# Delta stage of a hybrid decoder layer: a second tile for the output gate, the inverse's 64-blocks in turns, query norms from matmuls with ones

## The chip, the cores and the metric

The kernel runs on one core of one Trainium2 chip. The metric is device time in microseconds (us), the median of three runs. Engines are named as in the profile: PE is TensorE's matmuls, PEld its weight loads, DVE is VectorE, ACT ScalarE, POOL GpSimd, and SP the engine that issues most DMAs. Each engine works through its own instructions in order and waits on semaphores for the others.

## The reference

One layer in fp32 on 1024 prompt rows and 8 single decode rows: a combined projection, a gated delta rule (8 heads of 128, chunks), sliding-window attention, two gated branches, and a convolutional feed-forward net. What the change touches is the delta rule of the prompt:

```python
q = _l2norm(q) * (GDN_DK ** -0.5)
k = _l2norm(k)
...
m = jnp.where(strict, jnp.einsum('bhnik,bhnjk->bhnij', kb, k) * gam, 0.0)
t_inv = lax.linalg.triangular_solve(eye + m, jnp.broadcast_to(eye, m.shape),
                                    left_side=True, lower=True, unit_diagonal=True)
...
def step(S, inp):
    u_n, w_n, a_n, qd_n, kd_n, last_n = inp
    v_new = u_n - jnp.einsum('bhck,bhkv->bhcv', w_n, S)
    o = jnp.einsum('bhck,bhkv->bhcv', qd_n, S) + jnp.einsum('bhij,bhjv->bhiv', a_n, v_new)
    S = S * last_n[..., None, None] + jnp.einsum('bhck,bhcv->bhkv', kd_n, v_new)
    return S, o
```

The output o is RMS-normed and multiplied by silu of an output gate, which is one more projection.

## The kernel before

The kernel has five stages: start (to 90 us), attention (to 406), the delta rule (to 1125), the branches (to 1420) and the feed-forward net (to 2084). Every large product is one `mm`: three matmuls (L180, L181, L182) of split operands (wh, wl for the weights, b1h, b1l for the activations), 384 or 264 columns each. DVE makes wl (L130) and ACT wh (L129).

The delta stage uses chunks of 128 rows, so a head h of 8 has 8 chunks n. For each head three generators run:

- `delta_prepare`: K and Q transposed on PE (L190, `tp<-ident,K`, `tp<-ident,Q`), four transposes a burst, two bursts for each. ACT squares each transposed chunk and sums it along the free axis (L888, `osq`), which gives the squared norms `n2`. DVE scales the transposed K into `kd` (L890). Then the products K K and Q K (L906, L907), and V transposed and scaled into `vn` (L918).
- `unit_inverse`: the inverse `W` of each chunk's unit triangular matrix. Blocks of 16 are inverted by a loop on DVE (L1019, L1020, tile `T`), go through DRAM (`T<-wd`), and are turned by DVE (L1034, `MR`). Then the blocks are joined on PE: to 32 by L1038 and L1044 (quarters of 32x32), to 64 by L1056 and L1061, to 128 by L1070 and L1074 (64x64 blocks). L1070 fills the PSUM tile `zp` for all eight chunks, ACT copies it to `Zb` (L1071), L1074 fills `qp`, and ACT copies that into `W` (L1075).
- `delta_scan`: a chain over n. A step is `rc<-S,K` (L947, PE), `y` (L948, DVE), `rc<-y,W` (L950, PE), `s` (L952, ACT), `rc<-s,kd` (L954, PE), and the new S (L963, DVE); beside it L957 and L958 add up `o`. After n = 3 and n = 7 ACT squares four chunks of o (L969), DVE and POOL make a factor of the sums (L971, L972, and `power` at L125), DVE writes the normed o over `vn` (L976), PE turns vn (L190, `rc<-ident,vn`, "the turning of vn"), and DVE multiplies it into the gate's tile `sg` (L983), which SP stores to `oa` (L988).

Beside these run projections as filler: `delta_gate(h)` (an mm into th, then `sg`, L858 and L859), `delta_project(h + 2)` (mm, then the conv of K, Q and V on DVE: L784 once, L786 three times for each, L792 twice, with a tanh on ACT, L791), and projections of the branch gates. `weave` (L1258) gives each generator priorities: the inverse from 0, the scan from 100, delta_prepare of the next head from 250, filler from 100000. The program's scheduler then places each instruction on its engine by these priorities, by when its inputs are ready in its own model of time, and by when a tile's room is free; what it chooses is fixed, and each engine runs its list in order. `sg` has one buffer for heads 0 to 6, and head 7 borrows the room of a `z` tile. A pool's room is fixed for its life; constants that are not in `KEPT` are in the pool `cp2`, which lives on.

Of the kernel before, what the change touches and what calls it, by code (L numbers as in the profile page):

```python
# [12 lines left out]
AF = mybir.ActivationFunctionType  # L13
ALU = mybir.AluOpType
# [4 lines left out]
P = 128  # L19
NP = 1024  # L20
NS = 8
NT = NP + NS
KC = 8
H = 8
NCH = 8
FT = 22
CONV_W = 3072
EPS = 1e-6
# [5 lines left out]
HALF = [(0, 512), (512, 520)]  # L34
QW = 260
KEPT = {"ident", "ones", "mhalf", "phalf", "vecs", "fcw", "mT", "a2"}
COL_GATE, COL_BETA, COL_SQ = 3072, 4096, 4112
COL_SK, COL_SV, COL_GA, COL_GB = 5136, 5392, 5648, 6672


def bc(ap, dim, n):

    a = ap.unsqueeze(dim)
    shape = list(a.shape)
    shape[dim] = n
    return a.broadcast_to(shape)
# [18 lines left out]
class Step:  # L65
# [28 lines left out]
        return pool.tile(shape, dt, tag=tag, name=f"{tag}_{self.n}", **kw)  # L94

    def const(self, shape, name, dt=F32):
        pool = self.cp if name in KEPT else self.cp2
        return pool.tile(shape, dt, tag=name, name=name)


# [749 lines left out]
    def delta_gate(self, pa, pool, h):  # L850

        nc = self.nc
        sg = self.t(pool, [P, NT], "sg", bufs=1) if h + 1 < H else self.t(self.pz, [P, NT + 3], "z")[:, :NT]

        def gate_out(t, ps):
            lo, n = PARTS[t]
            th = self.t(pa, [P, 512], "th", bufs=2)[:, :n]
            nc.scalar.activation(th, ps, AF.Tanh, scale=0.5)  # L858
            nc.vector.scalar_tensor_tensor(sg[:, lo:lo + n], th, 1.0, ps, op0=ALU.add, op1=ALU.mult)  # L859

        self.project(self.win(COL_GATE + h * P), self.h, gate_out)
        nc.gpsimd.tensor_copy(self.sgs[:, h, :], sg[:, NP:NT])
        self.sg[h] = sg
        yield

    def delta_prepare(self, pool, psum, h):
        nc = self.nc
        K, Q, V = self.kqv[h]
# [45 lines left out]
        for c0 in (0, 4):  # L914
            tp = self.t(psum, [P, 4, P], "tp", bufs=2)
# [74 lines left out]
    def unit_inverse(self, pool, psum, h, U):  # L990

        nc, W = self.nc, self.W
# [7 lines left out]
        for p in range(4):  # L1000
            c = slice(16 * (p % 2), 16 * (p % 2) + 16)
# [8 lines left out]
        U64, Zb = UZ[0:64], UZ[64:128]  # L1010
# [12 lines left out]
        for p in range(4):  # L1023
            q, c = 16 * (p % 2) + 8 * (p // 2), slice(16 * (p % 2), 16 * (p % 2) + 16)
# [5 lines left out]
        TT = self.t(pool, [P, 2, NCH, 32], "MR", bufs=1)  # L1030
# [4 lines left out]
        zp = self.t(psum, [P, NCH, 32], "tp", bufs=2)  # L1035
# [5 lines left out]
        qp = self.t(psum, [P, NCH, 32], "tp", bufs=2)  # L1041
# [24 lines left out]

        nc.vector.transpose(flat(TT[32:64, 0]), flat(w01))
        zp = self.t(psum, [P, NCH, 2, 32], "tp", bufs=2)
        for n in range(NCH):
            nc.tensor.matmul(zp[64:128, n], U64[:, n, :], TT[0:64, :, n, :], start=True, stop=True)  # L1070
        nc.scalar.copy(Zb, zp[64:128].rearrange("p n a i -> p n (a i)"))  # L1071
        qp = self.t(psum, [64, NCH, 64], "tp", bufs=2)
        for n in range(NCH):
            nc.tensor.matmul(qp[:, n, :], Zb[:, n, :], W[64:128, n, 64:128], start=True, stop=True)  # L1074
        nc.scalar.copy(W[0:64, :, 64:128], qp)  # L1075


    def conv_states(self, pool, psum):
# [872 lines left out]

    def run(self):
        S, nc = ExitStack, self.nc
        self.constants()
        with S() as ca:
            with S() as c:
                pool, psum = self.pool("p2", 1, ctx=c), self.pool("q2", 1, PSUM, ctx=c)
                for tag, bufs in dict(qst=8, raw=2, kh=2, kl=2, E=3, obt=2, pp=2, pc=2, o=2).items():
                    self.bufs[id(pool), tag] = bufs
# [33 lines left out]
            with S() as c:  # L1993
                pa, pool, psum = self.pool("pa", 1, ctx=c), self.pool("p4", 1, ctx=c), self.pool("q4", 1, PSUM, ctx=c)
# [27 lines left out]
        with S() as c:  # L2022
            pool2, pool = self.pool("p6b", 1, ctx=c), self.pool("p6", 1, ctx=c)
# [48 lines left out]
```

## Time and profile before

| | us |
|---|---|
| median of three runs | 2083.78 |
| the runs | 2090.38, 2083.78, 2079.47 |
| span of the profiled execution | 2084.4 |
| PE busy in the span | 2012.7 |
| DVE busy | 1347.8 |
| ACT busy | 900.2 |
| POOL busy | 520.2 |

The profile is of one execution. A group's row has the line, engine and operation, out<-in by tile names, shape and count, then busy us and the mean ns of one, then the idle time of the engine just before its instructions and what ended it. A row of the timeline has start, duration, line and count of a run of like instructions, and in brackets the idle time before and what released it. Durations of pipelined matmuls overlap; from start to start is what one costs. An fp32 matmul is two records in the profile (x2) and one row in the order below.

### The profile page before, as it was taken

The page shows a single profiled execution, that of the slowest core. Times are in us where ns is not written, and L with a number is a line of the kernel's source. Part 1 is how long each engine was busy: PE and PEld are TensorE (multiplying, and loading weights), DVE is VectorE, ACT ScalarE, POOL GpSimd, SP SyncE. Part 2 cuts the span into 40 slices and gives each one's busy share as a digit, 9 for nine tenths or more (in the row PEclk, how much of TensorE's full clock was granted, in tenths as well). Part 3 has the DMA queues.
Part 4 walks back from the last instruction along what each step waited for, and adds up shares of the span by engine and source line. Part 5 has one row for each costly group of instructions (what it writes and reads, how often), then busy time and mean ns, then how long its engine had stood idle before and what let it go on. Part 6 is the DMA issues. An engine that isn't in the chain of part 4 may idle for free.

```text
span 2084.4 us, 41297 instructions
## 1 busy us (share of the span) xinstructions
PE 2012.7 (97%) x16245; PEld 1910.2 (92%) x16245; DVE 1347.8 (65%) x2714; ACT 900.2 (43%) x2233; POOL 520.2 (25%) x594
## 2 busy tenths in 40 slices
PE   7999998999999999989989999999999999999897
PEld 4987877799999999989989999999999999999897
DVE  5755768473655647656544675578876776767756
ACT  4664545433344243432342542354444444534443
POOL 2000000121321221201111000005575466446421
PEclk9999999999999999999999999999999999999999
DMA  8256443331332322312275855323333333488862
GB/s 300 62 144 210 135 167 116 117 94 51 80 80 61 73 72 52 89 42 62 63 223 172 285 186 163 112 63 97 105 91 112 102 92 112 136 305 266 291 215 94
DMA packets 301887, 275.75 MB, mean 132 GB/s; under 512 B 59730, under 2 KB 248111, under 8 KB 301676
## 3 DMA queue, kind: packets, MB, share of 16 engines
q1 hardware_dynamic: 295642, 252.14, 39.6%
q0 software_dynamic: 5552, 20.37, 2.8%
q8 instruction: 127, 2.08, 0.4%
q14 instruction: 68, 0.56, 0.1%
q10 hardware_dynamic: 498, 0.61, 0.1%
HBM read 212.93 MB, written 62.51 MB: 132 GB/s over the span
## 4 chain that ended last, share of the span: by engine, by line
PE 83%; DVE 5%; DMA 5%; ACT 3%; issue 1%; SPq 1%; POOL 1%; DVEq 0%; POOLq 0%; ACTq 0%
PE mm L180 19%; PE mm L181 18%; PE mm L182 18%; PE wv L180 3%; PE wv L182 3%; PE wv L181 3%; PE wy L182 2%; PE wy L180 2%; PE wy L181 2%; PE pv L652 1%; PE pt L190 1%; PE tp L190 1%; DVE x L1472 1%; PE mm L264 1%; PE rc L954 1%
## 5 line engine op out<-in xcount | busy, mean ns | idle before, releaser
L180 PE MATMUL mm<-b1h,wh 128*128 128x384 f32 (+1 forms) x1520 | 496.9, 328 | 3.7 <-ACT gt L1294 1.6
L181 PE MATMUL mm<-b1l,wh 128*128 128x384 f32 (+1 forms) x1520 | 489.3, 323 | 0.0
L182 PE MATMUL mm<-b1h,wl 128*128 128x384 f32 (+1 forms) x1520 | 488.0, 323 | 0.3 <-DVE wl L130 0.3
L180 PEld LDWEIGHTS mm<-b1h,wh 128*128 128x128 f32 x1520 | 286.7, 189 | 12.4 <-issue 4.6
L181 PEld LDWEIGHTS mm<-b1l,wh 128*128 128x128 f32 x1520 | 287.1, 189 | 4.4 <-issue 3.1
L182 PEld LDWEIGHTS mm<-b1h,wl 128*128 128x128 f32 x1520 | 286.3, 189 | 3.9 <-issue 2.8
L129 ACT ACTIVATE wh<-raw 128x1024 fp32r<-128x1024 f32 x83 | 87.0, 1049 | 122.4 <-PE mm L181 70.2
L130 DVE TENSOR_TENSOR wl<-raw,wh 128x1024 fp32r<-128x1024 f32 x82 | 101.0, 1233 | 57.2 <-ACT wh L129 55.1
L181 PE MATMUL mm<-pk,w 128*128 128x260 f32 (+1 forms) x440 | 124.8, 284 | 1.1 <-DVE pk L130 1.1
L180 PE MATMUL mm<-pk,w 128*128 128x260 f32 (+1 forms) x440 | 124.8, 284 | 0.0
L182 PE MATMUL mm<-pk,w 128*128 128x260 f32 (+1 forms) x440 | 124.5, 283 | 0.0
L130 DVE TENSOR_TENSOR w<-ws,w 128x512 fp32r<-128x512 f32 x88 | 78.0, 886 | 36.9 <-ACT w L129 36.7
L1626 ACT COPY bml<-mm 128x256 f32<-128x256 f32 (+1 forms) x132 | 48.9, 371 | 100.6 <-PE mm L182 96.7
L180 PE MATMUL mm<-bmh,w 128*128 128x260 f32 (+1 forms) x320 | 90.3, 282 | 0.0
L182 PE MATMUL mm<-bmh,w 128*128 128x260 f32 (+1 forms) x320 | 90.1, 282 | 0.0
L1681 DVE SCALAR_TENSOR_TENSOR fa<-fz,fcw,fa 128x512 f32<-128x512 f32 x88 | 75.2, 874 | 18.2 <-ACT fa L1679 17.9
L180 PE MATMUL mm<-b2h,wh 128*128 128x384 f32 (+1 forms) x256 | 83.2, 328 | 2.9 <-ACT wh L129 2.8
L181 PEld LDWEIGHTS mm<-pk,w 128*128 128x128 f32 x440 | 83.2, 189 | 1.3 <-DVE pk L130 1.3
L181 PE MATMUL mm<-b2l,wh 128*128 128x384 f32 (+1 forms) x256 | 83.6, 327 | 0.4 <-DVE b2l L130 0.4
L180 PEld LDWEIGHTS mm<-pk,w 128*128 128x128 f32 x440 | 83.2, 189 | 0.2 <-ACT bml L1626 0.2
L182 PEld LDWEIGHTS mm<-pk,w 128*128 128x128 f32 x440 | 83.4, 190 | 0.0
L182 PE MATMUL mm<-b2h,wl 128*128 128x384 f32 (+1 forms) x256 | 82.8, 326 | 0.0
(645 smaller groups left out, 5886.2 us busy)
## 6 DMA issues: line engine op xcount, KB each, us to landing
raw<-in_w_in_dram SPq DMA_DIRECT2D x59, 512.0 KB
ws<-in_w_ffn_down_dram SPq DMA_DIRECT2D x55, 256.0 KB
raw<-xd SPq DMA_DIRECT2D x47, 258.0 KB
raw<-in_w_ffn_down_dram SPq DMA_DIRECT2D x47, 256.0 KB
raw<-in_w_ffn_gate_dram SPq DMA_DIRECT2D x22, 512.0 KB
raw<-in_w_ffn_up_dram SPq DMA_DIRECT2D x22, 512.0 KB
qst<-in_w_mod_dram SPq DMA_DIRECT2D x16, 512.0 KB
raw<-in_w_mod_dram SPq DMA_DIRECT2D x16, 512.0 KB
```

Source lines behind the costliest of these rows:

```text
L129: self.nc.scalar.activation(hi, x, AF.Copy)
L130: (eng or self.nc.vector).tensor_tensor(lo, x, hi.bitcast(F32), op=ALU.subtract)
L180: mm(ps, whi, xhi, start=first, stop=False, **kw)
L181: mm(ps, whi, xlo, start=False, stop=False, **kw)
L182: self.last_mm = mm(ps, wlo, xhi, start=False, stop=last, **kw).ins
L190: self.nc.tensor.transpose(out, in_, self.ident[:p, :p])
L264: nc.tensor.matmul(ps[32 * j:32 * j + 32], self.cT[:, k0 + j, :], ws[j // 2][:, j % 2, :], start=k0 == 0, stop=k0 > 0)
L652: nc.tensor.matmul(pv[64 * r:64 * r + 64], V[:, n - back, ch], ps[:, r::2, :], start=back == 0, stop=back == (n > 0))
L954: yield step(nc.tensor.matmul(ds, kd[:, n, :], s, start=True, stop=True))
L1472: nc.vector.scalar_tensor_tensor(x[:, :np_], ps[:, :np_], by[:, j, 8:9], x[:, :np_], op0=ALU.mult, op1=ALU.add)
L1626: self.last_copy = nc.scalar.copy(r[p, i], x[p])
L1681: nc.vector.scalar_tensor_tensor(ai[:, c:e], zi[:, j + c:j + e], col(j), ai[:, c:e], op0=ALU.mult, op1=ALU.add)
```

## The change

It has three parts.

1. `sg` gets two buffers for all heads (L851 and its tile). The room comes from ten constants (`SHORT`), which go into a new pool `cp1` that closes after the attention.
2. In `delta_prepare`, the norms of Q no longer come from eight transposes. For four chunks at a time ACT squares Q as it lies (128 x 512, into the tile `ed`), four matmuls with a 128x32 part of `ones` sum it over the partitions, each for 32 of the rows of every chunk and onto its own 32 partitions, DVE turns the 32x32 blocks (128 x 128) and adds the small constant into `n2`. K's norms stay as they were.
3. In `unit_inverse`, L1070's and L1074's blocks are issued by fours: four chunks of zp, then four times a chunk of zp and one of qp in turn, then four of qp, with a copy for each four. `issue_after` keeps the second and third groups behind the copy before them.

```diff
+SHORT = {"triu", "tril", "trilu", "stril", "sink", "qs", "kx", "vx", "zero", "a1"}
...
-        pool = self.cp if name in KEPT else self.cp2
+        pool = self.cp if name in KEPT else self.cp1 if name in SHORT else self.cp2
...
-        sg = self.t(pool, [P, NT], "sg", bufs=1) if h + 1 < H else self.t(self.pz, [P, NT + 3], "z")[:, :NT]
+        sg = self.t(pool, [P, NT], "sg", bufs=2)
...
-        for a, src in ((0, K), (1, Q)):
-            for c0 in (0, 4):
-                tp = self.t(psum, [P, 4, P], "tp", bufs=2)
-                for c in range(4):
-                    self.transpose(tp[:, c, :], src[:, c0 + c, :])
-                junk = self.t(pool, [P, P], "osq", bufs=1)
-                for c in range(4):
-                    nc.scalar.activation(junk, tp[:, c, :], AF.Square, accum_out=n2[:, a, c0 + c:c0 + c + 1])
-                if a == 0:
-                    nc.vector.tensor_tensor(kd[:, c0:c0 + 4, :], tp, bc(self.edd[:, h, c0:c0 + 4], 2, P), op=ALU.mult)
-                yield
-        nc.vector.tensor_scalar_add(n2, n2, 4 * EPS)
...
+        nc.vector.tensor_scalar_add(n2[:, 0], n2[:, 0], 4 * EPS)
+        for c0 in (0, 4):
+            q2 = self.t(pool, [P, 4, P], "ed", bufs=1)
+            nc.scalar.activation(q2, Q[:, c0:c0 + 4, :], AF.Square)
+            sums = self.t(psum, [P, 4, 32], "tp", bufs=2)
+            for j in range(4):
+                r = slice(32 * j, 32 * j + 32)
+                nc.tensor.matmul(sums[r], self.ones[:, 0:32], q2[:, :, r], start=True, stop=True)
+            turned = self.t(pool, [P, 4, 32], "osq", bufs=1)
+            nc.vector.transpose(turned.rearrange("p n i -> p (n i)"), sums.rearrange("p n i -> p (n i)"))
+            nc.vector.tensor_scalar_add(n2[:, 1, c0:c0 + 4], turned[:, :, 0], 4 * EPS)
+            yield
...
-        for n in range(NCH):
-            nc.tensor.matmul(zp[64:128, n], U64[:, n, :], TT[0:64, :, n, :], start=True, stop=True)
-        nc.scalar.copy(Zb, zp[64:128].rearrange("p n a i -> p n (a i)"))
         qp = self.t(psum, [64, NCH, 64], "tp", bufs=2)
-        for n in range(NCH):
-            nc.tensor.matmul(qp[:, n, :], Zb[:, n, :], W[64:128, n, 64:128], start=True, stop=True)
-        nc.scalar.copy(W[0:64, :, 64:128], qp)
+        copied = None
+        for c0 in (0, 4, 8):
+            with self.tc.issue_after(copied) if copied else nullcontext():
+                for n in range(c0, c0 + 4):
+                    if n < NCH:
+                        nc.tensor.matmul(zp[64:128, n], U64[:, n, :], TT[0:64, :, n, :], start=True, stop=True)
+                    if c0:
+                        nc.tensor.matmul(qp[:, n - 4, :], Zb[:, n - 4, :], W[64:128, n - 4, 64:128], start=True, stop=True)
+            if c0 < NCH:
+                copied = nc.scalar.copy(Zb[:, c0:c0 + 4], zp[64:128, c0:c0 + 4].rearrange("p n a i -> p n (a i)")).ins
+            if c0:
+                nc.scalar.copy(W[0:64, c0 - 4:c0, 64:128], qp[:, c0 - 4:c0])
...
+                self.cp1 = self.pool("cp1", 1, ctx=c)
+                self.constants()
```

The scheduler's choice changes with it, in the delta stage only. Lines of the changed kernel: L180 to L182 become L181 to L183, L190 L191, L784 L785, L786 L787, L792 L793, L947 L957, L948 L958, L950 L960, L954 L964, L957 L967, L958 L968, L963 L973, L971 L981, L972 L982, L976 L986, L1034 L1044, L1038 L1048, L1044 L1054, L1056 L1066, L1061 L1071, L1070 L1085 and L1074 L1087; L898 is the matmul with ones.

The end of scan(5) on PE. The kernel before issues, ahead of the second turning of vn, the following; the first turning (`rc<-ident,vn`) stands 230 rows up, and 197 of the rows between are mm:

```order
L947 MATMUL rc_10744<-S_10741,K_8333 128x128
L957 MATMUL o_10700<-S_10741,Q_8334 128x128
...
L1070 MATMUL tp_11175<-MR_11055,UZ_10993 64x64 x2
L950 MATMUL rc_10747<-y_10743,W_4535 128x128
L1070 MATMUL tp_11175<-MR_11055,UZ_10993 64x64 x6
...
L954 MATMUL rc_10751<-s_10749,kd_9872 128x128
L958 MATMUL o_10700<-s_10749,A_9924 128x128
...
L1074 MATMUL tp_11185<-W_4535,UZ_10993 64x64 x8
L190 MATMUL tp_11942<-ident,K_10343 128x128 x4
L190 MATMUL tp_11953<-ident,K_10343 128x128 x4
L190 MATMUL rc_10766<-ident,vn_9957 128x128 x4
```

The rows left out there are mm: 30 ahead of the first L1070, 20 between L1070 and L954, 10 between L958 and L1074. In the changed kernel the first turning of the same scan stands behind three mm, and the inverse of head 6 begins behind it:

```order
L964 MATMUL rc_10695<-s_10693,kd_9886 128x128
L968 MATMUL o_10649<-s_10693,A_9938 128x128
L181 MATMUL mm_11461<-b1h_14_155,wh_11401 128x264
L182 MATMUL mm_11461<-b1l_15_156,wh_11401 128x264
L183 MATMUL mm_11461<-b1h_14_155,wl_11402 128x264
L191 MATMUL rc_10710<-ident,vn_9971 128x128 x4
L957 MATMUL rc_10718<-S_10699,K_8345 128x128
L967 MATMUL o_10716<-S_10699,Q_8346 128x128
L960 MATMUL rc_10721<-y_10717,W_4539 128x128
L1048 MATMUL tp_11074<-MR_11071,U_1757_11007 32x32 x24
```

From there to the second turning stand 34 rows and no mm. The end of them, in the changed kernel:

```order
L1085 MATMUL tp_11191<-MR_11071,UZ_11009 64x64 x4
L957 MATMUL rc_10760<-S_10757,K_8345 128x128
L967 MATMUL o_10716<-S_10757,Q_8346 128x128
L1085 MATMUL tp_11191<-MR_11071,UZ_11009 64x64 x4
L960 MATMUL rc_10763<-y_10759,W_4539 128x128
L964 MATMUL rc_10767<-s_10765,kd_9886 128x128
L968 MATMUL o_10716<-s_10765,A_9938 128x128
L1087 MATMUL tp_11192<-W_4539,UZ_11009 64x64 x4
L191 MATMUL tp_11960<-ident,K_10359 128x128 x4
L1087 MATMUL tp_11192<-W_4539,UZ_11009 64x64 x4
L191 MATMUL tp_11971<-ident,K_10359 128x128 x4
L191 MATMUL rc_10782<-ident,vn_9971 128x128 x4
```

The mm that stood here before stand in earlier heads. The four groups of the 64-blocks stand apart there, as they do in heads 1 to 6; the rows of L1085 and L1087 alternate in heads 0 and 7 alone, as here in head 0 of the changed kernel:

```order
L1085 MATMUL tp_5143<-MR_5023,UZ_4961 64x64
L1087 MATMUL tp_5144<-W_4539,UZ_4961 64x64
L1085 MATMUL tp_5143<-MR_5023,UZ_4961 64x64
L1087 MATMUL tp_5144<-W_4539,UZ_4961 64x64
L1085 MATMUL tp_5143<-MR_5023,UZ_4961 64x64
```

The end of scan(4) on DVE. Before, from the last y to vn, there are two conv rows of V's tanh:

```order
L948 SCALAR_TENSOR_TENSOR y_9741<-rc_9742,d_2591,vn_8949 128x128
L792 SCALAR_TENSOR_TENSOR v_1476_9343<-z_9534,v_1476_9343 128x512 x2
L963 SCALAR_TENSOR_TENSOR S_9753<-S_9739,d_2592,rc_9749 128x128
L971 TENSOR_SCALAR so_9629<-so_9629 128x4
L972 SCALAR_TENSOR_TENSOR so_9629<-n_1404_8865,so_9629 128x4
L976 TENSOR_TENSOR vn_8949<-o_9698,f_9630 128x512
```

In the changed kernel the same stretch, with the conv of the next K and Q in it (the first two rows after y, L785, stand ahead of these):

```order
L787 SCALAR_TENSOR_TENSOR K_10359<-z_10362,cw,K_10359 128x1024
L787 SCALAR_TENSOR_TENSOR Q_10360<-z_10457,cw,Q_10360 128x1024
L973 SCALAR_TENSOR_TENSOR S_9767<-S_9753,d_2595,rc_9763 128x128
L787 SCALAR_TENSOR_TENSOR K_10359<-z_10362,cw,K_10359 128x1024
L787 SCALAR_TENSOR_TENSOR Q_10360<-z_10457,cw,Q_10360 128x1024
L981 TENSOR_SCALAR so_9643<-so_9643 128x4
L787 SCALAR_TENSOR_TENSOR K_10359<-z_10362,cw,K_10359 128x1024
L787 SCALAR_TENSOR_TENSOR Q_10360<-z_10457,cw,Q_10360 128x1024
L982 SCALAR_TENSOR_TENSOR so_9643<-n_1412_8877,so_9643 128x4
L793 SCALAR_TENSOR_TENSOR K_10359<-z_10362,K_10359 128x512 x2
L793 SCALAR_TENSOR_TENSOR Q_10360<-z_10457,Q_10360 128x512
L986 TENSOR_TENSOR vn_8961<-o_9712,f_9644 128x512
```

With those two, eleven conv instructions stand ahead of vn where two stood. In head 7's inverse, the mm that stood between L1061 and L1070 are gone too.

More of the change, by code (lines that the diff above doesn't have):

```diff
@@ L880, in delta_prepare @@
         n2 = self.t(pool, [P, 2, NCH], "n2", bufs=2)
-        for a, src in ((0, K), (1, Q)):
-            for c0 in (0, 4):
-                tp = self.t(psum, [P, 4, P], "tp", bufs=2)
-                for c in range(4):
-                    self.transpose(tp[:, c, :], src[:, c0 + c, :])
-                junk = self.t(pool, [P, P], "osq", bufs=1)
-                for c in range(4):
-                    nc.scalar.activation(junk, tp[:, c, :], AF.Square, accum_out=n2[:, a, c0 + c:c0 + c + 1])
-                if a == 0:
-                    nc.vector.tensor_tensor(kd[:, c0:c0 + 4, :], tp, bc(self.edd[:, h, c0:c0 + 4], 2, P), op=ALU.mult)
-                yield
-        nc.vector.tensor_scalar_add(n2, n2, 4 * EPS)
+        for c0 in (0, 4):
+            tp = self.t(psum, [P, 4, P], "tp", bufs=2)
+            for c in range(4):
+                self.transpose(tp[:, c, :], K[:, c0 + c, :])
+            junk = self.t(pool, [P, P], "osq", bufs=1)
+            for c in range(4):
+                nc.scalar.activation(junk, tp[:, c, :], AF.Square, accum_out=n2[:, 0, c0 + c:c0 + c + 1])
+            nc.vector.tensor_tensor(kd[:, c0:c0 + 4, :], tp, bc(self.edd[:, h, c0:c0 + 4], 2, P), op=ALU.mult)
+            yield
+        nc.vector.tensor_scalar_add(n2[:, 0], n2[:, 0], 4 * EPS)
+        for c0 in (0, 4):
+            q2 = self.t(pool, [P, 4, P], "ed", bufs=1)
[7 more added lines that the diff above has]
+            nc.vector.tensor_scalar_add(n2[:, 1, c0:c0 + 4], turned[:, :, 0], 4 * EPS)
+            yield
         nk = self.t(pool, [P, NCH], "nk", bufs=2)
```

1 line of the change is left out of this document (removed).

## The prediction

> **What bounds the kernel now.** I read the page's totals first, then the table of busy time by stretches, then the timeline of TensorE in the delta stage. The totals:
>
> ```profile
> span 2084.4 us, 41297 instructions
> ...
> PE 2012.7 (97%) x16245; PEld 1910.2 (92%) x16245; DVE 1347.8 (65%) x2714; ACT 900.2 (43%) x2233; POOL 520.2 (25%) x594
> ```
>
> TensorE is busy 97% of the span, so time can be won in two ways only: less work on TensorE, or less of its 72 us of idle time. The table by stretches gives, for the delta stage, its first two thirds and the 89 us in which scan(4) ends and scan(5) begins, length, then busy time of PE, PEld, DVE, ACT, POOL, then granted clock:
>
> ```profile
> 406.00:1125.00 719.00, 699.55 (x6173) 674.73 (x6172) 417.74 (x889) 267.28 (x778) 133.08 (x186) 0.99 0.32 87
> 406.00:889.00 483.00, 478.71 (x4148) 465.40 (x4147) 288.88 (x611) 180.82 (x529) 101.12 (x137) 1.00 0.30 78
> 889.00:978.00 89.00, 83.60 (x726) 79.73 (x727) 55.41 (x117) 31.69 (x95) 11.23 (x19) 0.94 0.20 52
> ```
>
> The whole change lies in the delta stage, where TensorE idles 19.5 us of 719, and ACT and DVE have much room. A gain from idle time can therefore not pass 19.5 us. A loss has no such bound: the scan is a chain through PE, DVE and ACT, and it is cheap now only because projection matmuls (mm) stand between its steps. How well they cover shows where scan(5) ends:
>
> ```profile
> 1000.11 0.44 PE L1070 MATMUL tp<-MR,UZ 64*64 64x64 f32 x4
> 1000.49 0.49 PE L950 MATMUL rc<-y,W 128*128 128x128 f32 x2
> ...
> 1004.57 0.38 PE L954 MATMUL rc<-s,kd 128*128 128x128 f32 x2
> 1004.79 0.39 PE L958 MATMUL o<-s,A 128*128 128x128 f32 x2
> ...
> 1006.32 1.14 PE L1074 MATMUL tp<-W,UZ 64*64 64x64 f32 x16
> 1007.39 0.66 PE L190 MATMUL tp<-ident,K 128*128 128x128 f32 x4
> 1008.37 0.66 PE L190 MATMUL tp<-ident,K 128*128 128x128 f32 x4 [0.33 <-ACT W L1075]
> 1009.77 0.66 PE L190 MATMUL rc<-ident,vn 128*128 128x128 f32 x4 [0.74 <-DVE vn L976]
> ...
> 1011.70 0.49 PE L954 MATMUL rc<-s,kd 128*128 128x128 f32 x2 [0.48 <-ACT s L952]
> ```
>
> Here the three idle times are 0.33, 0.74 and 0.48 us, 1.6 together, because 197 rows of mm stand between the two transposes of vn, its turnings (the order above).
>
> **TensorE's own work: about +2.5 us.** The 64-blocks first. Of the rows above, four records of L1070 take 0.38 us to the next start and sixteen of L1074 1.07, so a record costs 0.058 and a burst some 0.15 besides. Before, a head has two bursts, 2.14 us. After, the order alternates L1085 and L1087 in heads 0 and 7 alone; in heads 1 to 6 the four groups of four (eight records each) stand apart with other work between: 4 x (0.15 + 8 x 0.058) = 2.45, +0.3 for each of six heads. Where they alternate, two quarters may run at once: three bursts of 0.61 make 1.84, -0.3 in each of two heads. Sum +1.2; from -2.4 (all eight won) to +2.5 (none).
>
> The Trainium skill, page "TensorEngine Tiling (Array Packing)", section Key Properties, says that a change of tiling mode, not of the tile alone, drains TensorE. It speaks against four bursts for two; the 0.15 us per burst agrees, and by the rule the sum stays +1.2.
>
> Query norms: eight transposes of Q in two bursts go, eight ones-matmuls on four column strips come. A burst of four transposes, and the nearest strip burst in the trace:
>
> ```profile
> 1012.25 0.60 PE L190 MATMUL tp<-ident,Q 128*128 128x128 f32 x4
> 1012.68 0.39 PE L947 MATMUL rc<-S,K 128*128 128x128 f32 x2
> ```
>
> ```profile
> 200.97 1.05 PE L264 MATMUL mm<-raw,cTr 128*32 128x512 f32 x4
> 201.95 0.33 PE L190 MATMUL pt<-ident,E 128*128 128x128 f32 x1
> ```
>
> The transposes hold TensorE for 0.43 us. Four strips of 512 columns held it for 0.98; a quarter of the columns is 0.25, and with a burst's 0.15 and as much for the way back 0.4 to 0.5. I take +1.3 for the sixteen bursts, from -3 (0.25 each) to +8 (strips one after another, eight records of 0.11 each, 0.9). On ACT, which has 450 us to spare in the stage, and DVE, 300 us, what goes and comes is hidden while mm stands beside it. Sum on TensorE: **+2.5**.
>
> **What the order moves: the large term.** With two sg tiles, a head's gate projection needs not wait until the head before has stored its tile, so the filler is issued earlier, and later heads have less. No time is won where it now stands: up to 889 us, the inverse of head 5, TensorE idles 4.3 us in 483 as it is. I credit -1. Where it is missing:
>
> *End of scan(5).* The rows of mm between the two turnings of vn fall from 197 to none, and three before the first. What is left is the chain. Its lengths come from the barest steps:
>
> ```profile
> 914.77 0.49 PE L947 MATMUL rc<-S,K 128*128 128x128 f32 x2
> 915.09 0.39 PE L957 MATMUL o<-S,Q 128*128 128x128 f32 x2
> 916.23 0.49 PE L950 MATMUL rc<-y,W 128*128 128x128 f32 x2 [0.75 <-DVE y L948]
> 917.48 0.49 PE L954 MATMUL rc<-s,kd 128*128 128x128 f32 x2 [0.77 <-ACT s L952]
> ...
> 1097.97 0.38 PE L954 MATMUL rc<-s,kd 128*128 128x128 f32 x2
> 1098.19 0.39 PE L958 MATMUL o<-s,A 128*128 128x128 f32 x2
> 1099.15 0.38 PE L947 MATMUL rc<-S,K 128*128 128x128 f32 x2
> 1100.11 0.38 PE L950 MATMUL rc<-y,W 128*128 128x128 f32 x2
> ```
>
> From L947 to L950 1.46 (0.96 at the best), from L950 to L954 1.25, from L954 to the next L947 1.18: 3.4 to 3.9 for a step, 3.6 taken. From a group's last L958 to its vn, by ACT, POOL and DVE:
>
> ```profile
> 1006.72 0.19 ACT L969 ACTIVATION_READ_ACCUMULATOR osq<-o 128x1 f32 x1
> ```
>
> ```profile
> 1007.46 1.02 POOL L125 TENSOR_TENSOR f<-so,mhalf 128x4 f32<-128x4 f32 x1 [4.16 <-DVE so L972]
> ```
>
> ```profile
> 1009.03 0.68 DVE L976 TENSOR_TENSOR vn<-o,f 128x512 f32<-128x512 f32 x1
> ```
>
> L958 at 1004.79, transposes at 1009.77: 5.0 us. The bare chain, from the first group's L968 to the second turning of vn, is 5.0 + 0.5 (turning, then the next step) + 4 x 3.6 + 5.0 = 25. TensorE's work in it, by the spacings quoted: 3 mm 0.4, vn and K turned 3 x 0.43 = 1.3, four steps of five matmuls at 0.22 to 0.33 = 4.6, the 64-blocks 2.45, the 16- and 32-blocks four bursts of the 0.68 us that one of them shows here, 2.7: 11.5.
>
> ```profile
> 640.76 0.75 PE L1038 MATMUL tp<-MR,U 32*32 32x32 f32 x64
> 641.44 0.45 PE L180 MATMUL mm<-b1h,wh 128*128 128x384 f32 x1
> ```
>
> Idle 13.5, less the 1.6 of before: **+12**. It can be more by what the inverse adds: S of the first step stands on DVE behind the inverse's transpose, which waits for a round trip through DRAM, and had it wait 2.94 us in head 5:
>
> ```profile
> 888.41 0.45 DVE L1034 STREAM_TRANSPOSE MR<-T 128x256 f32<-128x256 f32 x1 [2.94 <-DMA T<-wd]
> ```
>
> It can be less if the inverse's matmuls come just where a step waits better than I count, or if vn starts when POOL ends, at 1008.48, and not at 1009.03. Range 8 to 18.
>
> *End of scan(4).* The order puts eleven conv instructions of the next K and Q between the last y and vn on DVE. Their prices, and the way from y to vn as it is now:
>
> ```profile
> L786 DVE SCALAR_TENSOR_TENSOR K<-z,cw,K 128x1024 f32<-128x1024 f32 x21 | 27.1, 1289 | 0.1
> ```
>
> ```profile
> L792 DVE SCALAR_TENSOR_TENSOR K<-z,K 128x512 f32<-128x512 f32 x14 | 9.3, 681 | 2.0 <-ACT z L791 2.0
> ```
>
> ```profile
> 915.83 0.34 DVE L948 SCALAR_TENSOR_TENSOR y<-rc,d,vn 128x128 f32<-128x128 f32 x1
> ...
> 923.07 0.69 DVE L976 TENSOR_TENSOR vn<-o,f 128x512 f32<-128x512 f32 x1 [1.19 <-POOL f L125]
> ```
>
> Six of L787 at 1.29, two of L785 at 0.75 (an estimate from the L786 row, without its second input), three of L793 at 0.68, then S, so and vn, 1.4 together, make 12.7 us from y to vn, where the rows show 7.9 (915.83 to 923.76). Behind vn's transposes, first to wait in PE's queue, stands all of scan(5). PE has beside it three scan matmuls, both L1087 groups, both K bursts and twenty mm, some 5 us: idle 7.5, against 2.4 in the same stretch now (0.77 and 1.61). Of the +5 I take **+3**, since more mm stands ahead of it after the change (the waits of scan(4) now, 0.75 and those ahead, can go); range 0 to 8.
>
> *The inverse of head 7* loses the mm between L1071 and L1085. What an uncovered hand-over there costs, and what follows an idle time:
>
> ```profile
> 919.81 1.97 PE L1074 MATMUL tp<-W,UZ 64*64 64x64 f32 x16 [1.61 <-ACT W L1065]
> ```
>
> That is **+1.5** (0 to 3).
>
> *The clock.* The same sixteen matmuls take 1.97 us here and 1.14 at 1006.32, in a stretch whose granted clock is 0.94 (the 889 row above) after some 5 us of idle time: 6% of 83.6 busy us is 5 us at the most, much of it beside waits. For stretches idle three times as long in all I take **+3** (0 to 6). The Trainium skill, page "TensorE: Matmul & The Clock Gate", Part 1, says that the clock falls to half after an idle window of about 3.4 us and comes back after a busy window of the same length. By that rule three long idle times would each cost some 1.7 us behind them, 5 in all, and the time would be 2107; the 0.94 agrees with a gate that closes, though no single idle time of before is 3.4 us long.
>
> Sum: 2.5 - 1 + 12 + 3 + 1.5 + 3 = **+21** on the profiled execution's span of 2084.4 us, 2105. The median of the three runs, 2083.78, stands within 1 us of that span, so I leave it at that.
>
> **The rivals.**
>
> *Work saved and no cover lost (faster).* Strips run four at once (-3), quarters pair wherever they meet (-0.3 for two heads, or up to -2.4), and the mm moved ahead fills the waits at 889 to 927 (6 us), while the chain at the end of scan(5) runs under what PE has anyway. It decides if a bare step takes not 3.6 but about 2.3 us and vn comes 3 after its group: then the chain is 0.5 + 4 x 2.3 + 2 x 3 = 15.7 long against 11.5 of work, and 4 - 1.6 = 2.6 us are lost there. Time 2084 - 3 - 1 - 6 + 2.6 = 2077. For it: the two 5 us waits for vn have other engines idle beside them, so they may shrink. Against it: the rows quoted give no bare step under 3.4. Chance 0.14.
>
> *No difference that shows.* The chain at the end of scan(5) costs 5 rather than 12, the conv queue ahead of vn is done early, the tail keeps its cover: +2 to +10, 2086 to 2094. For it: the idle rows sit beside estimates of cover that I made from counts of rows. Chance 0.24.
>
> *Strips one after another.* Eight records of 0.11 a burst and no overlap: +8 in place of +1.3, 2112. The L264 row speaks against it: four records of 512 columns in 0.98, where at L958's 0.22 for two records of 128 they would take 1.8 one after another. Chance 0.10, part of slower.
>
> *The change does not do what it says.* For the 64-blocks it does not in six heads of eight; that is in the sum at +1.2, and alone (were the order otherwise as before) would leave 2087. It counts among no difference.
>
> **How the numbers follow.** A measurement of this kernel tells about 0.5% from no change, 10.4 us. The forecast, +11 to +33 without serial strips, has 0.52; with these slower has 0.62, same 0.24, faster 0.14. The bounds of the terms, -3 to +10.5 for PE's work, 8 to 18, 0 to 8, 0 to 3 and 0 to 6, do not all fall one way: the likeliest case's own range is 2096 to 2118. For 8 in 10 the range reaches up to 2122 (strips serial, or scan(5) at 18) and down to 2080, so that it takes in no difference and the milder half of faster.
>
> **What would show it.** In the profile after: PE busy in the delta stage up by 1 to 4 us and its idle time from 19.5 to about 35; one idle time of 4 to 7 us ahead of "rc<-ident,vn" at each of the two turnings of scan(5), released by vn; idle times of 1 us or so at each step between; one of 5 to 8 us before the last turning of scan(4); granted clock of these stretches under 0.95; L1085 and L1087 in bursts of eight records of about 0.6 us in heads 1 to 6, and the L898 burst at 0.4 to 0.5 us. From the branches on, nothing. The forecast is wrong if idle time in the delta stage stays under 25 us, or if the steps at the end of scan(5) run at 2.5 us without mm between them.

## The result and the profile after

The changed kernel takes 2117.3 us (median of 6 runs, 2114.13 to 2119.39) against 2085.36 us for the kernel before (median of 6 runs beside it). The ratio is 1.0148 with a 95% interval of 1.0129 to 1.0167: slower by about 31 us.

The totals of the page of the changed kernel:

```profile
span 2116.8 us, 41365 instructions
...
PE 2029.5 (96%) x16309; PEld 1920.4 (91%) x16309; DVE 1358.3 (64%) x2746; ACT 889.1 (42%) x2137; POOL 530.3 (25%) x594
```

Against 2084.4 and 2012.7 before, the span grew by 32.4 us: TensorE is idle 87.3 us in place of 71.7, +15.6, and busy +16.8. So half of the loss does not appear as idle time at all. Where the two halves lie, the table of busy time by stretches shows. It has length, busy time of PE, PEld, DVE, ACT and POOL, granted clock, DMA share and GB/s. First the kernel before, cut at the end of scan(4) and the end of scan(5):

```profile
406.00:905.00 499.00, 493.16 (x4372) 478.74 (x4371) 296.50 (x622) 184.18 (x537) 101.22 (x138) 1.00 0.29 77
905.00:928.00 23.00, 19.37 (x158) 17.09 (x157) 12.65 (x21) 14.15 (x51) 2.40 (x4) 0.85 0.15 49
1005.00:1012.00 7.00, 5.46 (x48) 4.43 (x47) 4.47 (x8) 6.43 (x30) 1.02 (x1) 1.00 0.28 80
1012.00:1125.00 113.00, 104.77 (x911) 99.65 (x910) 57.50 (x138) 37.72 (x101) 17.02 (x24) 0.98 0.56 160
```

And the changed kernel, cut at the same places of the program:

```profile
406.00:945.00 539.00, 535.87 (x4660) 516.61 (x4661) 312.59 (x659) 184.66 (x479) 107.13 (x143) 1.00 0.29 75
945.00:971.00 26.00, 20.26 (x186) 17.32 (x185) 16.75 (x30) 13.65 (x47) 5.13 (x4) 0.80 0.01 3
1008.30:1047.00 38.70, 27.91 (x308) 22.49 (x306) 15.35 (x43) 13.89 (x53) 2.95 (x4) 0.56 0.12 30
1047.00:1160.00 113.00, 99.80 (x869) 95.11 (x862) 58.06 (x141) 34.75 (x88) 18.61 (x26) 0.94 0.61 171
```

Up to the end of scan(4) the idle time falls from 5.8 to 3.1 us. There it is 5.7 against 3.6. At the end of scan(5) it is 10.8 against 1.5, and the clock is 0.56 over 38.7 us. Behind it, it is 13.2 against 8.2. The delta stage as a whole is longer by 35.0 us, with 13.4 us more idle and 21.6 us more busy time; the stages behind it are shorter by 2.6 us together:

```profile
406.00:1160.00 754.00, 721.13 (x6278) 688.48 (x6279) 427.91 (x931) 257.61 (x686) 144.18 (x189) 0.96 0.32 86
```

Some of the longest waits of PE in the delta stage, in us in total, times, and longest:

```profile
PE rc L191 <- DVE vn L986: 8.2, 2, 6.8
PE mm L181 <- DVE gt L1342: 4.3, 2, 3.6
PE tp L1087 <- ACT W L1075: 2.7, 2, 1.6
PE mm L181 <- ACT z L781: 2.7, 1, 2.7
```

The first is the turning of vn, 6.8 us of it in scan(5). The last stands at the end of scan(4). The timeline of PE at the end of scan(5) shows both halves:

```profile
1008.14 0.39 PE L968 MATMUL o<-s,A 128*128 128x128 f32 x2
...
1015.69 1.12 PE L191 MATMUL rc<-ident,vn 128*128 128x128 f32 x4 [6.79 <-DVE vn L986]
...
1017.91 0.80 PE L960 MATMUL rc<-y,W 128*128 128x128 f32 x2 [0.25 <-DVE y L958]
1020.06 0.86 PE L1048 MATMUL tp<-MR,U 32*32 32x32 f32 x48 [1.35 <-DVE MR L1044]
...
1024.19 0.80 PE L960 MATMUL rc<-y,W 128*128 128x128 f32 x2
...
1029.70 0.80 PE L960 MATMUL rc<-y,W 128*128 128x128 f32 x2
...
1035.34 0.79 PE L960 MATMUL rc<-y,W 128*128 128x128 f32 x2
...
1043.54 1.06 PE L191 MATMUL rc<-ident,vn 128*128 128x128 f32 x4
```

PE waits 6.79 us for vn. From then on the matmuls of the chain take twice their time (0.80 for a pair that took 0.38), and a step, from L960 to L960, is 6.3, 5.5 and 5.6 us long. The first has an idle time of 1.35 us in it, the third one of 0.21, the second none. The stretch from L968 to the second turning is 35.4 us.

That vn came so late has its reason on DVE: ACT had the last sum of squares at 1010.95, but DVE took up `so` (L981) only at 1013.40, behind the end of the inverse's loop and a `wl`:

```profile
1012.32 1.15 DVE L131 TENSOR_TENSOR wl<-raw,wh 128x1024 fp32r<-128x1024 f32 x1
```

TensorE's own work can be read where the clock is full. Two quarters at once in head 0, eight records alone, and the norms:

```profile
496.51 0.27 PE L1085 MATMUL tp<-MR,UZ 64*64 64x64 f32 x1
...
497.12 0.44 PE L183 MATMUL mm<-b1h,wl 128*128 128x384 f32 x1
```

```profile
577.76 0.68 PE L1085 MATMUL tp<-MR,UZ 64*64 64x64 f32 x8
578.37 0.39 PE L183 MATMUL mm<-b1h,wl 128*128 128x264 f32 x1
```

```profile
605.42 0.43 PE L898 MATMUL tp<-ed,ones 128*32 128x128 f32 x8
605.78 0.49 PE L916 MATMUL tp<-K 128*128 128x128 f32 x2
```

Sixteen alternating records take 0.61 us, and so do eight alone: two quarters do run at once. A burst of norms takes 0.36, as four strips side by side would. On top of each burst of tiles comes about 0.1 us on entry (mm to L1085 0.21 at 577.55, mm to mm of the same width 0.12). So a head with four bursts pays 4 x 0.71 against 2 x 1.17, +0.5, six times; heads 0 and 7 gain 0.2 each; the norms pay 16 x 0.1: +4 us in all. As much again is lost on leaving (the mm behind that burst, at 578.37, holds TensorE for 0.22 in place of 0.12). With that, and with 0.08 that the transposes of Q lost on leaving too, the same sum makes about +6, so I take 4 to 6.

### The profile page after: what moved, and what is told of

It reads as the page before. It is cut to its first block, busy times and chain, and to the rows that moved or that the text cites. A ratio compares the mean times of both kernels' runs of the same rounds, so it can differ in the third digit from the quotient of the medians.

```text
span 2116.8 us, 41365 instructions
## 1 busy us (share of the span) xinstructions
PE 2029.5 (96%) x16309; PEld 1920.4 (91%) x16309; DVE 1358.3 (64%) x2746; ACT 889.1 (42%) x2137; POOL 530.3 (25%) x594
## 4 chain that ended last, share of the span: by engine, by line
PE 42%; DMA 7%; DVE 6%; ACT 2%; SPq 1%; issue 1%; POOL 1%; DVEq 0%; POOLq 0%; ACTq 0%
PE mm L181 9%; PE mm L182 9%; PE mm L183 9%; PE wv L181 2%; PE wv L182 2%; PE wv L183 2%; DMA ws<-in_w_ffn_down_dram 1%; PE wy L183 1%; PE wy L181 1%; PE wy L182 1%; DMA bmh<-in_w_ffn_down_dram 1%; DMA raw<-in_w_ffn_down_dram 1%; DMA b1l<-dlr 1%; DVE pk L131 1%; DMA raw<-in_w_o_dram 1%
## 5 line engine op out<-in xcount | busy, mean ns | idle before, releaser
L181 PE MATMUL mm<-b1h,wh 128*128 128x384 f32 (+1 forms) x1520 | 491.2, 329 | 8.8 <-DVE gt L1342 4.3
L182 PE MATMUL mm<-b1l,wh 128*128 128x384 f32 (+1 forms) x1520 | 485.1, 324 | 0.0
L183 PE MATMUL mm<-b1h,wl 128*128 128x384 f32 (+1 forms) x1520 | 482.4, 323 | 0.0
L181 PEld LDWEIGHTS mm<-b1h,wh 128*128 128x128 f32 x1520 | 286.2, 190 | 17.5 <-issue 5.4
L182 PEld LDWEIGHTS mm<-b1l,wh 128*128 128x128 f32 x1520 | 286.5, 190 | 4.8 <-issue 3.3
L183 PEld LDWEIGHTS mm<-b1h,wl 128*128 128x128 f32 x1520 | 285.8, 189 | 4.2 <-issue 3.2
L131 DVE TENSOR_TENSOR wl<-raw,wh 128x1024 fp32r<-128x1024 f32 x82 | 101.6, 1239 | 72.3 <-ACT wh L130 71.7
L182 PE MATMUL mm<-pk,w 128*128 128x260 f32 (+1 forms) x440 | 124.7, 284 | 1.1 <-DVE pk L131 1.1
L181 PE MATMUL mm<-pk,w 128*128 128x260 f32 (+1 forms) x440 | 124.6, 283 | 0.0
L183 PE MATMUL mm<-pk,w 128*128 128x260 f32 (+1 forms) x440 | 124.5, 283 | 0.0
L181 PE MATMUL mm<-bmh,w 128*128 128x260 f32 (+1 forms) x320 | 90.2, 282 | 0.0
L183 PE MATMUL mm<-bmh,w 128*128 128x260 f32 (+1 forms) x320 | 90.1, 282 | 0.0
L181 PE MATMUL mm<-b2h,wh 128*128 128x384 f32 (+1 forms) x256 | 84.3, 330 | 5.7 <-ACT wh L130 3.9
L182 PE MATMUL mm<-b2l,wh 128*128 128x384 f32 (+1 forms) x256 | 84.4, 330 | 0.4 <-DVE b2l L131 0.4
L182 PEld LDWEIGHTS mm<-pk,w 128*128 128x128 f32 x440 | 83.1, 189 | 1.3 <-DVE pk L131 1.3
L181 PEld LDWEIGHTS mm<-pk,w 128*128 128x128 f32 x440 | 83.2, 189 | 0.2 <-ACT bml L1642 0.2
L183 PEld LDWEIGHTS mm<-pk,w 128*128 128x128 f32 x440 | 83.3, 190 | 0.0
L183 PE MATMUL mm<-b2h,wl 128*128 128x384 f32 (+1 forms) x256 | 83.1, 327 | 0.0
```

What stands on the lines that cost most here:

```text
L131: (eng or self.nc.vector).tensor_tensor(lo, x, hi.bitcast(F32), op=ALU.subtract)
L181: mm(ps, whi, xhi, start=first, stop=False, **kw)
L182: mm(ps, whi, xlo, start=False, stop=False, **kw)
L183: self.last_mm = mm(ps, wlo, xhi, start=False, stop=last, **kw).ins
```

## The experiments

Each ran beside the kernel before on one chip. The two columns on the right compare the profiled execution with that of before (span less PE busy, 71.7; PE busy, 2012.7). They are of one execution each, which need not be the median: that of part 3 alone is the longest of its five (2101.29 against a median of 2096.51), that of parts 2 and 3 is 2.4 us under its median. The busy time of the two kernels with added matmuls holds these, about 6.5 and 16 us from start to start.

| kernel | ratio, 95% interval | idle us | busy us |
|---|---|---|---|
| the whole change | 1.0148 (1.0129 to 1.0167) | +15.6 | +16.8 |
| part 1 alone | 1.0103 (1.0072 to 1.0134) | +12.1 | +13.0 |
| part 2 alone | 1.0070 (1.0050 to 1.0090) | +7.4 | +9.9 |
| part 3 alone | 1.0044 (1.0030 to 1.0059) | +5.9 | +9.3 |
| parts 2 and 3 | 1.0051 (1.0033 to 1.0069) | +5.3 | +5.0 |
| eight matmuls in the wait | 1.0124 (1.0105 to 1.0142) | +8.1 | +21.5 |
| gate held back | 1.0121 (1.0101 to 1.0142) | +14.1 | +15.1 |
| matmuls in all waits | 1.0156 (1.0137 to 1.0176) | +6.9 | +20.7 |
| one more piece early | 1.0164 (1.0145 to 1.0184) | +15.5 | +15.8 |
| parts 2 and 3, other priority | 1.0076 (1.0054 to 1.0097) | +4.6 | +9.8 |
| other priority alone | 1.0042 (1.0028 to 1.0055) | +3.1 | +3.5 |

**Part 1 alone.**

```diff
-        sg = self.t(pool, [P, NT], "sg", bufs=1) if h + 1 < H else self.t(self.pz, [P, NT + 3], "z")[:, :NT]
+        sg = self.t(pool, [P, NT], "sg", bufs=2)
```

(with the pool cp1 that makes the room)

> The kernel before with part 1 alone (two sg tiles, short-lived constants). Theory A, the second gate tile takes the cover from the end of scan(5): its order has no mm between the two turnings of vn in scan(5), as the whole change has, so it loses nearly all of what the whole change loses, +25 to +32 us (2110 to 2117), with a granted clock of about 0.5 behind the first turning. Theory B, the norms and the split 64-blocks cost it: within 5 us of the kernel before.

About +21 us by the ratio, somewhat under theory A's 25 and far from B's 5. The signature is A's: at the end of scan(5) PE waits 6.99 us (for the inverse's MR here), and the clock stays at 0.50:

```profile
1011.25 0.86 PE L1039 MATMUL tp<-MR,U 32*32 32x32 f32 x46 [6.99 <-DVE MR L1035]
```

```profile
1010.00:1020.00 10.00, 8.75 (x179) 7.56 (x180) 4.03 (x9) 0.91 (x3) 0.00 (x0) 0.50 0.19 56
```

So part 1 by itself, with no operation added, makes most of the loss. The pool `cp1` came with the second tile and was not run alone, so this run does not part the two; nothing waits for the pool that shows, since from 406 to 929 us PE idles 0.01 us in all.

**Part 2 alone.**

```diff
+                nc.tensor.matmul(sums[r], self.ones[:, 0:32], q2[:, :, r], start=True, stop=True)
```

(with the rest of part 2)

> The kernel before with part 2 alone (norms of Q by ones). Its order keeps 187 rows of mm between the turnings of scan(5). Theory A: -3 to +4 us, 2082 to 2089. Theory B (strips one after another, +8, and moved order): +8 us or more.

**Part 3 alone.**

```diff
+        for c0 in (0, 4, 8):
+            with self.tc.issue_after(copied) if copied else nullcontext():
```

(with the rest of part 3)

> The kernel before with part 3 alone (64-blocks by fours). Theory A: 0 to +4 us (four bursts for two in six heads, +1.2). Theory B (the uncovered hand-overs of four groups are the loss): +10 us or more, with idle time ahead of L1074's place in most heads.

**Parts 2 and 3 without part 1.**

```diff
-        sg = self.t(pool, [P, NT], "sg", bufs=2)
+        sg = self.t(pool, [P, NT], "sg", bufs=1) if h + 1 < H else self.t(self.pz, [P, NT + 3], "z")[:, :NT]
```

> The changed kernel without part 1 (one sg tile again, norms and 64-blocks as changed). Theory A: -2 to +6 us against the kernel before, 2083 to 2091, mean granted clock back at 0.99. Theory B: +25 us or more.

Theory A missed in all three: +15, +9 and +11 us, where I had left 4 to 6. Nor was it B's mechanism for the norms, since a burst takes 0.36 us, nor for the 64-blocks: ahead of L1077, L1074's place in part 3 alone, PE waits 1.8 us in all, in two places. Together parts 2 and 3 cost no more than part 2 alone. Prices of operations would add; these don't. Idle time rises in each, and busy time with it, also in part 3 alone, whose own work is under 1 us of its +9.3: in its order the rows alternate in six heads and not in two. Which waits make the loss in each of the three was not followed up.

**Other priority alone, and with parts 2 and 3.** These two ask whether an order of the same instructions can cost that much.

```diff
-                        streams.append((self.delta_prepare(pool, psum, h + 1), 250, 1))
+                        streams.append((self.delta_prepare(pool, psum, h + 1), 500, 1))
```

> The kernel before with that priority at 500 alone: not one instruction is added or taken away. Theory A, the order by itself sets 10 us: +4 to +16 us with more idle time in the delta stage. Theory B, an order with as many mm in each half of a scan costs nothing: within 3 us of the kernel before.

> The changed kernel without part 1 and with the priority of the next head's delta_prepare at 500 in place of 250: the same instructions as in the run without part 1, in another order, no half of a scan with fewer mm than the kernel before has. Theory A, parts 2 and 3 cost their own work (+3.9 us by the bursts' measured spacing) and the rest of that run's +12 is what its order happens to leave uncovered: between +2 and +20 us, and the difference to the run without part 1 follows idle time and clock. Theory B, the parts cost +12 whatever the order: +10 to +14.

The kernel before, with no instruction added, loses 9 us by that line, clear of noise: theory A. Parts 2 and 3 go from +11 to +16, but the two intervals overlap, so that run does not decide between its theories. In the first, PE's longest waits are again the hand-overs of scan and inverse:

```profile
PE rc L954 <- ACT s L952: 6.7, 7, 3.5
PE tp L1074 <- ACT UZ L1071: 3.9, 2, 2.5
```

**One more piece early.** The kernel before with filler spent sooner, and no part of the change.

```diff
-                        streams.append((self.pieces(3), 10000, 100))
+                        streams.append((self.pieces(4), 10000, 100))
```

> The kernel before, none of the three parts, with one more piece of branch-gate projection in each of heads 0 to 5 (four for three). Total work is the same; the order has 45 and no rows of mm in scan(7)'s halves where there were 99 and 81. Theory A, what costs is filler spent early and missing late: idle time in the delta stage up by 10 to 20 us, the clock at 0.5 there for 20 us or more, +15 to +35 us (2100 to 2120). Theory B, the loss is tied to the gate's tile and not to where the filler stands: within 5 us of the kernel before.

Theory A held: +34 us, idle +15.5 and busy +15.8, nearly the numbers of the whole change, with one gate tile. The bare place is now the end of scan(7), where the order has no mm left, at half clock:

```profile
1140.00:1150.00 10.00, 8.28 (x32) 6.70 (x31) 2.91 (x7) 0.73 (x2) 0.00 (x0) 0.54 0.00 0
1150.00:1160.00 10.00, 3.86 (x13) 2.68 (x12) 3.66 (x10) 2.57 (x10) 4.66 (x7) 0.50 0.60 203
```

```profile
1156.60 1.12 PE L190 MATMUL rc<-ident,vn 128*128 128x128 f32 x4 [3.96 <-DVE vn L976]
```

**Gate held back.** The changed kernel, with the projection of a gate placed behind the store of the head before.

```diff
-        self.project(self.win(COL_GATE + h * P), self.h, gate_out)
+        with self.tc.issue_after(self.stored) if self.stored else nullcontext():
+            self.project(self.win(COL_GATE + h * P), self.h, gate_out)
...
-        queue.dma_start(self.oa[h][:, 0:NP], sg[:, 0:NP])
+        self.stored = queue.dma_start(self.oa[h][:, 0:NP], sg[:, 0:NP]).ins
```

> The changed kernel, two sg tiles kept, but the scheduler may place a head's gate projection only behind the store of the head before. In its order 197 mm stand again between the turnings of scan(5). Theory A, the second tile costs only by letting the filler run ahead: time near the kernel without part 1, +4 to +14 us against before (2090 to 2100), idle time in the delta stage 20 to 26 us. Theory B, the second tile or the closed pool costs by itself (room, stores, waits): 2110 or more.

A miss: the cover at the end of scan(5) is back, and yet it loses 25 us. The time range was B's, but PE's waits are not for room or stores; they are spread over the scans' hand-overs:

```profile
PE rc L965 <- ACT s L963: 7.9, 7, 2.3
PE rc L961 <- DVE y L959: 6.3, 8, 1.6
PE tp L1088 <- ACT W L1076: 4.2, 3, 1.6
```

The filler is a fixed sum. Held back by this rule it is missing in other heads: in the two halves from scan(3)'s first turning to scan(4)'s first, the trace has 150 and 186 matmuls of mm, where the kernel before has 179 and 225, and PE idles 4.9 us in place of 0.6. What the one tile did before was to ration it in a way that fits; a second rule that only looks alike does not.

**Eight matmuls in the wait.** To part the idle time from the half clock behind it.

```diff
+                if h == 5 and n == 3:
+                    for _ in range(8):
+                        nc.tensor.matmul(tp.rearrange("p c i -> p (c i)"), K[:, n, :],
+                                         K[:, 0:4, :].rearrange("p n i -> p (n i)"), start=True, stop=True)
                 for c in range(4):
                     self.transpose(tp[:, c, :], vn[:, c0 + c, :])
```

> The changed kernel with eight more matmuls of 128x512 (results overwritten, about 7 us) behind L968 of n = 3 in scan(5), where TensorE idles 6.8 us for vn; all else in the same order. Theory A, the idle time closes the clock and the half clock then draws out the bare chain for 30 us: granted clock stays near 1.0 behind it, the steps of scan(5) take about 3.6 us and not 5.5, and the time falls by 6 to 12 us to about 2107. Theory B, the chain through ACT and DVE alone sets those steps: granted clock up, steps still 5 us or more, time unchanged or up to 2 us longer (2117 to 2120). Theory C, the small matmuls let the clock fall anyhow: clock 0.5 again within some 5 us behind the turning, time unchanged.

Theory C, as far as it goes: time unchanged. The wait for vn was filled, but the order on DVE moved too, y behind the inverse's transpose, so that PE waited there, and the clock was at half again from 1019.2 us. It fell with that wait of 2.73 us, so this run does not show that the small matmuls alone let it fall, as theory C has it:

```profile
1019.28 0.64 PE L1052 MATMUL tp<-MR,U 32*32 32x32 f32 x28 [2.73 <-DVE MR L1048]
```

```profile
1018.69 0.45 DVE L1048 STREAM_TRANSPOSE MR<-T 128x256 f32<-128x256 f32 x1 [4.55 <-DMA T<-wd]
```

**Matmuls in all waits of scan(5).** Eleven in that place, and more in each step:

```diff
+            for _ in range(4 if h == 5 and n > 3 else 0):
+                nc.tensor.matmul(sp, K[:, n, :], K[:, n, :], start=True, stop=True)
             yield step(nc.tensor.matmul(sp, W[:, n, :], y, start=True, stop=True))
...
+            for _ in range(3 if h == 5 and n > 3 else 0):
+                nc.tensor.matmul(ds, K[:, n, :], K[:, n, :], start=True, stop=True)
             yield step(nc.tensor.matmul(ds, kd[:, n, :], s, start=True, stop=True))
```

> The changed kernel with matmuls of no use wherever scan(5) waits from n = 3 on: eleven of 128x512 ahead of the turning of vn (about 9.7 us, the two waits of 1013 to 1019), then four of 128x128 ahead of each L960 and three ahead of each L964 (0.9 and 0.7 us a step). In the run with eight alone the clock was 0.5 again from 1020 us, after a wait of 2.7 us. Theory A, the half clock draws the chain out: if the clock stays at 0.9 or more through the chain, steps take 3.6 to 4.2 us in place of 5.5, the stretch from L968 of n = 3 to the second turning 29 to 31 us in place of 36, and the time is 2107 to 2112. Theory B, the chain is set by ACT, DVE and the inverse's round trip: clock up, stretch 35 us or more, time as before or longer (2115 to 2122).

Now the clock held, up to 1038 us (from there to 1045, behind waits of 0.93, 0.17 and 0.46 us, it was at half), and the steps are shorter:

```profile
1010.00:1020.00 10.00, 10.00 (x82) 6.09 (x82) 3.63 (x8) 1.42 (x2) 1.02 (x1) 1.00 0.16 22
1020.00:1030.00 10.00, 10.00 (x207) 8.88 (x205) 2.84 (x8) 2.20 (x6) 0.00 (x0) 1.00 0.18 54
```

```profile
1006.60 0.39 PE L972 MATMUL o<-s,A 128*128 128x128 f32 x2
1006.82 9.61 PE L996 MATMUL rc<-K 128*128 128x512 f32 x22
...
1018.92 0.39 PE L962 MATMUL rc<-y,W 128*128 128x128 f32 x2
...
1023.71 0.49 PE L962 MATMUL rc<-y,W 128*128 128x128 f32 x2
...
1027.82 0.49 PE L962 MATMUL rc<-y,W 128*128 128x128 f32 x2
...
1032.41 0.49 PE L962 MATMUL rc<-y,W 128*128 128x128 f32 x2
...
1040.12 1.11 PE L191 MATMUL rc<-ident,vn 128*128 128x128 f32 x4 [0.70 <-DVE vn L990]
```

L960's steps (L962 here) take 4.8, 4.1 and 4.6 us where they took 6.3, 5.5 and 5.6. That part is theory A's. But the stretch, from L972 (L968 above), is 33.5 us against 35.4, between the two theories, because the first step begins 12.3 us behind the group's end and not 9.8. And the kernel's time is unchanged: 1.0156 against 1.0148, inside each other's intervals. By the second turning of scan(6), in the profiled executions, it was 6 us ahead; by the first of scan(7) it had lost all but 1.4 of them. There PE waits behind DVE, and DVE for a small read, `gt<-sgb`, while the DMA engines carry 300 GB/s, in the changed kernel (first) and here:

```profile
1103.62 0.43 DVE L1342 TENSOR_TENSOR gt<-mm,gt 128x264 f32<-128x264 f32 x1 [5.02 <-DMA gt<-sgb]
```

```profile
1097.73 0.43 DVE L1350 TENSOR_TENSOR gt<-mm,gt 128x264 f32<-128x264 f32 x1 [6.15 <-DMA gt<-sgb]
...
1102.69 0.43 DVE L1350 TENSOR_TENSOR gt<-mm,gt 128x264 f32<-128x264 f32 x1 [3.25 <-DMA gt<-sgb]
```

That is one part. PE's own wait for `gt` is 2.31 us here and 3.63 there; more is lost behind it, at the hand-overs of head 7's inverse, where ACT has waited for a read of weights:

```profile
1106.10 1.06 ACT L130 ACTIVATE wh<-raw 128x1024 fp32r<-128x1024 f32 x1 [1.57 <-DMA raw<-in_w_swa_out_dram]
```

```profile
1107.60 0.36 PE L1093 MATMUL tp<-MR,UZ 64*64 64x64 f32 x1 [1.65 <-ACT UZ L1097]
```

The same wait of PE is 0.46 us in the changed kernel. So the half clock does lengthen the bare chain, but giving the clock back at this one place gives no time back.

## Why the prediction was right, and where it was short

The direction and the mechanism were right, most of the places too, and the time lies in the range, near its upper end; +21 was forecast and +32 came, on the profiled executions. The 11 us between them are busy time: 5.5 was forecast in the terms for TensorE's own work and the clock, 16.8 came.

- **What the order moves.** The idle time was forecast at -1, +12, +3 and +1.5, together +15.5; the profile has +15.6. That this agrees so well is luck: 13.4 of it lie in the delta stage, the other 2.2 outside, where nothing was forecast, and the terms are off both ways. By place: up to the end of scan(4) -2.7, there +2.1, at the end of scan(5) +9.3, behind it +5. The last has the 1.5 us of head 7's inverse (L1085 waits 1.0 and 0.5) and 3.6 us that no step of mine had, the wait for `gt` behind a full DMA. Part 1 alone and the kernel with one more early piece both show that filler spent early is enough for the loss.
- **End of scan(4).** The queue on DVE was read rightly: from y (953.27) to the end of vn (965.92) it took 12.7 us, as forecast. But PE filled the wait with mm, and its longest idle time there is 2.70 us, for the z of a projection, not one of 5 to 8 us for vn.
- **End of scan(5).** The first step that was too small: the bare chain, 25 us, took 35.4. Its first wait for vn was 7.5 us and not 5.0, since the inverse's loop and a `wl` stood on DVE, and its steps 5.5 to 6.3 and not 3.6. Of the two idle times of 4 to 7 us that were to show, the first came, 6.79 us; ahead of the second turning there was none, and those between the steps were 0.2 to 0.5 us but for one: at half clock the matmuls filled them. I took the steps from rows at full clock. With the clock held at full they are 4.1 to 4.8, still more than 3.6, with matmuls of no use in the queue.
- **The clock.** The second, and the larger: +3, from 0 to 6, where the busy time grew by 16.8 us, of which the operations explain 4 to 6. The other 11 to 13 are put down to half clock: in the delta stage PE is busy at 0.50 for 45.2 us (958 to 968, 1012.5 to 1046.6, 1104.6 to 1118.3), where it was for 12.0, and half of these 33 us is the most that a full clock could have saved. At the end of scan(5) alone the granted clock is 0.56 over 38.7 us, 17 us less than full, and the mechanism that I named reaches much further than the 5 us that I read from the stretch with 0.94. I treated it as a tail behind an idle time; it covers the whole chain, for as long as nothing but chain and inverse runs. That is also why PE's busy time in the delta stage, which was to grow by 1 to 4 us, grew by 21.6, some of it mm that had stood behind the stage (96 of these matmuls stand there, 125 before).
- **These two terms are one.** Chain and clock overlap: what a step takes at half clock would in part be waiting at full clock. The runs bound this only at scan(5), where at least 1.3 us a step depend on the clock. How much of the 11 to 13 us would be left as idle time if the clock held in all places was not settled, and whether it pays there is open as well, since what was gained at scan(5) was lost behind it, where DVE and ACT wait for reads.
- **TensorE's own work.** +2.5 was forecast, +4 to +6 measured; I left out the 0.1 us on entry of a burst and the 0.1 on leaving. Alternation in heads 0 and 7 alone, and four bursts of 0.61 in the others (1.04 at half clock), came as the order says. The strips run side by side. The lower bound of the term is misadded: -2.4 and -3 make -5.4, not -3.
- **What the forecast did not say**: that parts 2 and 3, at 4 to 6 us of work, cost 11, and that a changed priority alone costs 9. The uncertainty of an order was in my range as bounds of places that I had looked at; it belongs to every place.
- **The rivals.** Serial strips: no (0.36 us a burst). No lost cover: no (10.8 us idle at scan(5)). None of the kernels tried beats the kernel before.

## What to carry to other kernels

Where filler covers a dependent chain, a buffer's wait can be what rations the filler: before removing such a wait, count in the new order how much filler each stretch of the chain has left. Here the wait itself, DVE's for the store of `sg` in the kernel before, was 1.7 us in all:

```profile
L859 DVE SCALAR_TENSOR_TENSOR sg<-th,mm 128x384 f32<-128x384 f32 x14 | 7.2, 549 | 1.7 <-DMA oa<-sg 1.7
```

Price a bare chain at the clock that it will run at, not at the durations that its steps have under cover, and count on new busy time beside new idle time: here it was about one us for one. In this kernel, busy 97%, a change of order alone moved the time by 0.4%, 9 us, more than part 2 or part 3 was hoped to win (3 and 2.4 us at most), so parts must be timed by themselves and in more than one order.

## What the runs showed of the hardware

- The clock stayed at half although PE hardly paused: over ten microseconds of the bare chain the profile of the changed kernel has PE busy for 9.94.

```profile
1020.00:1030.00 10.00, 9.94 (x207) 8.47 (x208) 2.70 (x7) 1.47 (x4) 0.00 (x0) 0.50 0.01 3
```

  The Trainium skill, page "TensorE: Matmul & The Clock Gate", Part 1, has the clock come back after a busy window of about 3.4 us. These quarter tiles and 128-column matmuls do not agree: they show no wait from 1020.06 to 1030.74 us, and the clock stayed at half to 1046.6, if busy means busy by the profile, in which the ends of matmuls are modelled. With seven more small matmuls a step, and the wait ahead of it filled, the same chain ran at 1.00 up to 1038 us; that run shows a clock that is kept, not one that comes back.
- One wait of 2.73 us was enough for the clock to fall (to 0.50 at 1019.2 us, in the kernel with eight matmuls in the wait), behind 6.5 us of matmuls of 512 columns and some 2 us of others.
- Every kernel here gained busy time along with idle time: without any added work +13.0 beside +12.1, +15.8 beside +15.5, +3.5 beside +3.1.
- Sixteen records of 64x64 on two quarters in turn took 0.61 us, as long as eight on one.
